# Solve's columns dealt out in turn over the partition groups, and SSD's dt moved into an exponent

## The chip, the cores and the metric

The kernel runs on one core of a Trainium2 chip. The metric is the device time of one execution in microseconds; lower is better. It is written in a tile language: the program text issues instructions to five engines (TensorE `pe`, ScalarE `act`, VectorE `dve`, GpSimd `pool`, SyncE `sp`, which issues the DMAs), and a scheduler puts the instructions of each engine in one queue, which the engine works off in order.

## The reference

One inference step of a hybrid layer on 1024 prompt rows and 64 sample rows (1088 in all), width 1024, all float32. What matters here are two of its parts. The gated DeltaNet (8 heads) solves, for each chunk of rows, a unit lower triangular system:

```
kk = einsum('bhik,bhjk->bhij', kh, kh)
lhs = where(strict, kk * dec * bt[..., :, None], 0.0) + eye
sol = triangular_solve(lhs, rhs, left_side=True, lower=True, unit_diagonal=True)
```

The Mamba-2 scan (SSD, 32 heads in 8 groups) weights each pair of rows i, j of a chunk by a decay and by dt of row j:

```
dec = exp(where(causal, gam_t[..., :, None] - gam_t[..., None, :], -inf))
w = cb[:, :, None] * dec * dt_t[..., None, :]
y = einsum('bghij,bjghp->bighp', w, xc)
```

The rest of the layer is an input projection (1024 to 12336 columns), causal convolutions, gates, two branch projections, an output projection, and a convolutional feed-forward part.

## The kernel before

Activations lie with channels on the 128 partitions and the 1088 rows along the free axis. Every projection is a loop over 128-column weight tiles; a weight is split into a high and a low part (`split`: ScalarE rounds `whi`, L114, VectorE subtracts to `wlo`, L115), and three matrix products per block of 128 are summed in PSUM, for three segments of 364 rows, in three rotating PSUM tiles `pj`.

The first part (to about 1560 us) weaves the input projections with the two scans. `weave` is a planner on the host: it keeps a model of TensorE's time in `now`, tasks that yield the latency (`LAT`) after which they may go on, and whenever no task is due it lets the main loop issue the next projection. TensorE's order is the order of the program text (`MAN`); the other engines' queues are ordered by the scheduler. Projections of q, k, v, x, B and C run through a convolution (`conv_steps`, VectorE L519 and L522, ScalarE L509, L517, L521); those of the gate z leave through `fz` (ScalarE L891, VectorE L893) to DRAM.

`decays` runs once: it makes dt (`dt8`, dt/8 for SSD), the negated cumulative decays `ngam` and derived tables, with ScalarE's Exp and Ln.

`gdn_inverse(h)` inverts one head's triangular matrices, 9 chunks of 128 rows with 4 diagonal blocks of 32 rows each, 36 blocks. The 32x32 diagonal blocks are inverted on VectorE, which this text calls Solve (L636 to L645): the blocks go through DRAM (`dU`) so that 108 partitions hold them, 3 groups of 36 partitions; each group works on 11 of the 33 columns (32 and one of padding) of all 36 blocks. For i from 1 to 31 one product (L640, `prod`) and one reduction (L643) make row i of the first n columns, n = min(i, 11). Then `XT` is a transposed copy (L645), written to DRAM as `dXT` (L648), read back into `NU` (L654), and transposed (L656, `prod` again). TensorE then combines the blocks (products from `prod`, `NU` and `Ub`, tile `n`). The planner counts 74 us for all of it (`LAT["solve"]`). `gdn_scan(h)` goes over the chunks one after the other: `r` (VectorE, L736), `u` (ScalarE, L742), the state `st` (L752), and `kd`, `vt` (ScalarE, L720, L721) for the next chunk.

`ssd_mix(g)` handles one group of four SSD heads, nine chunks. `decay` loads the decay rows into `gi`, masks them on GpSimd (L817) and takes four Exp of 128x128 into `E` with the row's `ngam` as bias (L820). `inputs` puts C'B and three transposes into one PSUM tile `sa`; VectorE multiplies E by it (L834), ScalarE copies the transposed B to `bt` (L836), and VectorE makes `xd` = x dt (L840) and `xw` = x wj (L841). TensorE sums xd'E and the state's part into `sy`, which VectorE reads for the new state (L872) and for `yc` (L878).

The later parts (branch projections, output projection, feed-forward) are not touched.

Of the kernel before, what the change touches and what calls it, by code (L numbers as in the profile page):

```python
# [15 lines left out]
AF = mybir.ActivationFunctionType  # L16
ALU = mybir.AluOpType
# [3 lines left out]
P = 128  # L21
# [26 lines left out]
def body(tc, I, O):  # L48
    nc = tc.nc
    ctx = ExitStack()  # L50
    pe, act, dve, pool, sp = nc.tensor, nc.scalar, nc.vector, nc.gpsimd, nc.sync
# [269 lines left out]
    with ExitStack() as c1:  # L321
# [111 lines left out]
        ngam = tl(c1p, [P, NC, 40], "ngam")  # L433
        beta = tl(c1p, [P, NC, 8], "beta")
        dt8 = tl(c1p, [P, NC, 32], "dt8")
# [11 lines left out]
        def decays():  # L447
            def tmp48(t):
                return t[:, 0:NC * 48].rearrange("p (c k) -> p c k", k=48)
            pz = tl(pp, [P, NC, 48], "n")  # L450
            for c in range(NC):
                tr(pz[:, c, :], zr[0:48, c * P:(c + 1) * P], ident[0:48, 0:48])
            zz, s1, s2, s3 = (tmp48(sgt(t)) for t in ("bm", "cm", "x0", "x1"))
            dve.tensor_scalar(out=zz[:, :, 0:8], in0=pz[:, :, 0:8], scalar1=-1.0, scalar2=None, op0=ALU.mult)
            dve.tensor_tensor(out=zz[:, :, 8:48], in0=pz[:, :, 8:48],
                              in1=bias40.unsqueeze(1).to_broadcast([P, NC, 40]), op=ALU.add)

            dve.scalar_tensor_tensor(out=s1, in0=zz, scalar=-1.0, in1=zz, op0=ALU.mult, op1=ALU.max)
            act.activation(s1, s1, AF.Exp, scale=-1.0)
            dve.tensor_scalar(out=s2, in0=s1, scalar1=1.0, scalar2=None, op0=ALU.add)  # L460
            act.activation(s3, s2, AF.Ln)
            dve.scalar_tensor_tensor(out=s1, in0=s2, scalar=-1.0, in1=s1, op0=ALU.add, op1=ALU.subtract)
            act.activation(s2, s3, AF.Exp, scale=-1.0)
            dve.tensor_tensor(out=s1, in0=s1, in1=s2, op=ALU.mult)
            dve.tensor_tensor(out=s3, in0=s3, in1=s1, op=ALU.subtract)
            dve.scalar_tensor_tensor(out=zz, in0=zz, scalar=0.0, in1=s3, op0=ALU.max, op1=ALU.add)
            act.activation(beta, zz[:, :, 0:8], AF.Exp, scale=-1.0)
            lga = tmp48(tl(gp, [P, TC], "E"))[:, :, 0:40]
            dve.tensor_tensor(out=lga, in0=zz[:, :, 8:48], in1=na.unsqueeze(1).to_broadcast([P, NC, 40]), op=ALU.mult)
            dve.memset(lga[64:128, 8, :], 0.0)  # L470
            dve.tensor_scalar(out=dt8, in0=zz[:, :, 16:48], scalar1=0.125, scalar2=None, op0=ALU.mult)
            yield LAT["dec2"]
            pg = tl(pp, [P, NC, 40], "sa")
            mm(pg, tri, lga, True, True)
            act.mul(ngam, pg, -1.0)
            yield 1.5
            pg = tl(pp, [P, NC, 40], "sy")
            mm(pg, sel, ngam, True, True)
            act.activation(ebl, pg, AF.Exp, scale=-1.0)
            dve.tensor_tensor(out=el, in0=ngam, in1=pg, op=ALU.subtract)  # L480
            act.activation(el, el, AF.Exp)
            dve.scalar_tensor_tensor(out=wj, in0=dt8, scalar=2.0, in1=el[:, :, 8:40], op0=ALU.mult, op1=ALU.mult)
            act.activation(neg, ngam[:, :, 0:8], AF.Exp, scale=-1.0)
            dve.tensor_scalar(out=neg, in0=neg, scalar1=-1.0, scalar2=None, op0=ALU.mult)
            grow = tl(gp, [P, TC], "NU", bufs=2)
            for (s, e), tag in zip(SEG9, ("gk", "gs", "sa")):
                pr = tl(pp, [P, 512], tag)
                for c in range(s // P, e // P):
                    tr(pr[0:40, c * P - s:(c + 1) * P - s], ngam[:, c, :], ident)
                act.copy(grow[0:40, s:e], pr[0:40, :384])  # L490
            sp.dma_start(gdr, grow[0:40, :])
# [102 lines left out]
        def gdn_inverse(h):  # L594
# [8 lines left out]
            for c0 in range(0, NC, 4):  # L603
                n = min(4, NC - c0)
                ps = tl(pp, [P, 4, P], "n")
                for c in range(c0, c0 + n):
# [16 lines left out]
                                     op0=ALU.mult, op1=ALU.mult)  # L623
# [10 lines left out]
            X = tl(gp, [108, 32, 11], "Xb")  # L634
            sp.dma_start(X, I["xinit"])
            for i in range(1, 32):  # L636
                n = min(i, 11)
                pr = tl(gp, [P, NC * 64], "prod")[0:108]
                prv = pr[:, 0:n * (i + 1)].rearrange("p (c j) -> p c j", j=i + 1)
                dve.tensor_tensor(out=prv, in0=X[:, 0:i + 1, 0:n].rearrange("p j c -> p c j"),  # L640
                                  in1=U[:, 0:i + 1, i:i + 1].rearrange("p j o -> p o j").to_broadcast([108, n, i + 1]),
                                  op=ALU.mult)
                dve.tensor_reduce(out=X[:, i, 0:n], in_=prv, axis=mybir.AxisListType.X, op=ALU.add)  # L643
            XT = tl(gp, [P, NC * 64], "prod")[0:108, 0:352].rearrange("p (c j) -> p c j", j=32)
            dve.tensor_copy(XT, X.rearrange("p j c -> p c j"))  # L645
            dXT = tl(dr, [NC * 4, 33, 32], "dXT", bufs=2)
            for g in range(3):
                sp.dma_start(dXT[:, 11 * g:11 * g + 11], XT[36 * g:36 * g + 36])  # L648
            dXv = dXT.rearrange("(c b) j i -> c b j i", b=4)

            Tl = tl(gp, [P, NC * 64], "prod").rearrange("p (c i) -> p c i", i=64)
# [155 lines left out]
        def ssd_mix(g):  # L807
# [3 lines left out]
            d4 = slice(4 * g, 4 * g + 4)  # L811

            def decay(c):
                gi = tl(sg, [P, 4, P], "gi", bufs=2)
                sp.dma_start(gi, gdr[h4, c * P:(c + 1) * P].partition_broadcast(P))
                E = tl(sg, [P, 4, P], "E", bufs=2)
                pool.affine_select(out=E, in_=gi, pattern=[[0, 4], [1, P]], compare_op=ALU.is_ge, fill=-NEG,  # L817
                                   base=0, channel_multiplier=-1)
                for a in range(4):
                    act.activation(E[:, a, :], E[:, a, :], AF.Exp, bias=ngam[:, c, 8 + 4 * g + a:9 + 4 * g + a], scale=-1.0)  # L820
                if c > 0:
                    act.activation(gi, gi, AF.Exp, scale=-1.0)
                    dve.scalar_tensor_tensor(out=gi, in0=chunk(cm, c).unsqueeze(1).to_broadcast([P, 4, P]),
                                             scalar=0.5, in1=gi, op0=ALU.mult, op1=ALU.mult)
                return gi, E

            def inputs(c, dec_c):

                gi, E = dec_c
# [7 lines left out]
                xd = tl(sg, [P, 4, 64], "xd", bufs=2)  # L837
                xw = tl(sg, [P, 4, 64], "xw", bufs=2)
                xv = ps[:, 2:4, :].rearrange("p a (b q) -> p (a b) q", q=64)
                dve.tensor_tensor(out=xd, in0=xv, in1=dt8[:, c, d4].unsqueeze(2).to_broadcast([P, 4, 64]), op=ALU.mult)  # L840
                dve.tensor_tensor(out=xw, in0=xv, in1=wj[:, c, d4].unsqueeze(2).to_broadcast([P, 4, 64]), op=ALU.mult)  # L841
                return gi, E, bt, xd, xw
            s8 = tl(sg, [P, 4, 64], "s8")
# [399 lines left out]
def layout(i):  # L1243
# [14 lines left out]
    def chans(a):  # L1258
# [5 lines left out]
    d = {  # L1264
        "ident": np.eye(P, dtype=np.float32),
        "tri": np.triu(np.ones((P, P), np.float32)),
        "xinit": np.tile(np.eye(32, 33, dtype=np.float32).reshape(1, 32, 3, 11).transpose(2, 0, 1, 3), (1, 36, 1, 1))
                   .reshape(108, 32, 11),
        "sel": np.concatenate([np.zeros((P - 1, P), np.float32), np.ones((1, P), np.float32)]),
        "xT": np.concatenate([g["x_prompt"][0], g["x_sample"][0]]).T.reshape(KT, P, T),  # L1270
# [61 lines left out]
```

## Time and profile before

| | |
|---|---|
| median of 3 runs | 2805.5 us (2805.27 to 2807.74) |
| the profiled execution | 2797.74 us, its span 2795.9 us |
| TensorE busy | 2728.5 us (98%), 18650 products |
| VectorE busy | 1868.0 us (67%), 3982 instructions |
| ScalarE busy | 1235.1 us (44%), 2813 instructions |
| GpSimd busy | 191.2 us (7%) |
| granted TensorE clock, mean | 0.996 of full speed |

The span runs from the first to the last instruction; the execution's own time has 1.8 us more around it. Busy time of TensorE is counted over pipelined products whose ends are modelled, so 98% does not mean that every cycle does work; what can be read safely is where TensorE stands idle and for whom. "Idle before, releaser" names the instruction whose end let a waiting one start. A number behind an arrow is the time waited.

### The profile page before, as it was taken

The numbers are of one execution on the slowest core, as the hardware profiler recorded it, in microseconds if no ns is written. First come the engines' busy times: TensorE is split into PE (matmuls) and PEld (weight loads), VectorE is DVE, ScalarE is ACT, GpSimd is POOL, SyncE is SP. The second block draws the span as 40 slices with busy tenths as digits, with TensorE's granted clock in tenths as the row PEclk, the third lists the DMA queues.
The fourth block names the chain that finished last, engine by engine and source line by source line (L and its number), as shares of the span: only waits on it lengthen the run. The fifth ranks groups of instructions, "written<-read, shape, count | busy, mean of one in ns | idle before, by whom it ended". The sixth has DMA issues, their size and how long they took to land.

```text
span 2795.9 us, 48799 instructions
## 1 busy us (share of the span) xinstructions
PE 2728.5 (98%) x18650; PEld 2639.7 (94%) x18650; DVE 1868.0 (67%) x3982; ACT 1235.1 (44%) x2813; POOL 191.2 (7%) x565
## 2 busy tenths in 40 slices
PE   6999999999999999999999999999999999999998
PEld 6999998999999999999999999999899999999998
DVE  5777679697887978877544557543666464555556
ACT  5634455454555545544443334222544242424244
POOL 0100001011110101101000000000000000000000
PEclk9999999999999999999999999999999999999999
DMA  6222323223231322323125755343211111111112
GB/s 228 95 67 88 112 68 107 79 79 106 71 120 61 110 76 84 100 76 107 65 92 202 262 188 185 122 144 93 87 53 46 46 41 43 46 42 50 39 61 73
DMA packets 204075, 266.72 MB, mean 95 GB/s; under 512 B 42490, under 2 KB 136378, under 8 KB 203842
## 3 DMA queue, kind: packets, MB, share of 16 engines
q1 hardware_dynamic: 203842, 263.62, 29.0%
q8 instruction: 146, 2.39, 0.3%
q14 instruction: 87, 0.71, 0.1%
HBM read 217.38 MB, written 46.13 MB: 94 GB/s over the span
## 4 chain that ended last, share of the span: by engine, by line
PE 81%; DVE 9%; DMA 5%; ACT 2%; issue 1%; POOL 1%; SPq 0%; DVEq 0%; POOLq 0%; ACTq 0%
PE pj L226 30%; PE pj L147 16%; PE sy L147 6%; PE sa L147 6%; PE gk L147 5%; PE gs L147 5%; PE sy L226 3%; DVE prod L640 2%; DMA gi<-gdr 2%; DVE Xb L643 2%; PE n L226 1%; DMA wada<-in_wada 1%; PE gk L226 1%; PE gs L226 1%; PE pj L1217 1%
## 5 line engine op out<-in xcount | busy, mean ns | idle before, releaser
L226 PE MATMUL pj<-h,whi 128*128 128x364 f32 x4560 | 1152.2, 334 | 5.8 <-DVE fz L893 5.8
L226 PEld LDWEIGHTS pj<-h,whi 128*128 128x128 f32 x4560 | 792.5, 189 | 13.5 <-DVE fz L893 7.0
L226 PE MATMUL pj<-h,wlo 128*128 128x364 f32 x2280 | 748.1, 328 | 3.8 <-DVE wlo L115 3.8
L147 PE MATMUL pj<-op,whi 128*128 128x364 f32 (+1 forms) x1904 | 476.7, 330 | 0.8 <-ACT op L188 0.6
L226 PEld LDWEIGHTS pj<-h,wlo 128*128 128x128 f32 x2280 | 429.0, 188 | 4.1 <-DVE wlo L115 4.1
L114 ACT CAST whi<-wraw 128x512 fp32r<-128x512 f32 (+1 forms) x382 | 231.2, 616 | 368.3 <-PE pj L147 130.7
L147 PEld LDWEIGHTS pj<-op,whi 128*128 128x128 f32 x1904 | 337.3, 188 | 6.7 <-issue 1.4
L115 DVE TENSOR_TENSOR wlo<-wraw,whi 128x512 fp32r<-128x512 f32 (+1 forms) x382 | 258.1, 685 | 102.2 <-ACT whi L114 101.4
L147 PE MATMUL pj<-op,wlo 128*128 128x364 f32 (+1 forms) x952 | 312.5, 329 | 0.0
L1124 DVE SCALAR_TENSOR_TENSOR acc<-buf,wfc,acc 128x364 f32<-128x364 f32 (+1 forms) x264 | 156.6, 597 | 96.5 <-ACT acc L1122 92.4
L147 PEld LDWEIGHTS pj<-op,wlo 128*128 128x128 f32 x952 | 178.8, 188 | 0.0
L147 PE MATMUL sy<-op,whi 128*128 128x364 f32 (+1 forms) x672 | 167.8, 330 | 0.0
L147 PE MATMUL gs<-op,whi 128*128 128x364 f32 (+1 forms) x652 | 164.1, 331 | 0.9 <-ACT q L1001 0.7
L147 PE MATMUL sa<-op,whi 128*128 128x364 f32 (+1 forms) x644 | 161.4, 330 | 0.0
L147 PE MATMUL gk<-op,whi 128*128 128x364 f32 (+1 forms) x640 | 159.5, 330 | 0.7 <-ACT op L114 0.7
L640 DVE TENSOR_TENSOR prod<-Xb,Ub 108x2 f32<-108x2 f32 (+30 forms) x248 | 129.2, 521 | 3.4
L820 ACT ACTIVATE E<-E,ngam 128x128 f32<-128x128 f32 x288 | 94.5, 394 | 74.2 <-POOL E L817 74.1
L147 PEld LDWEIGHTS sy<-op,whi 128*128 128x128 f32 x672 | 119.0, 188 | 1.0 <-issue 0.4
L147 PEld LDWEIGHTS gs<-op,whi 128*128 128x128 f32 x652 | 115.5, 188 | 3.1 <-ACT q L1001 0.9
L147 PEld LDWEIGHTS sa<-op,whi 128*128 128x128 f32 x644 | 114.0, 188 | 1.2 <-issue 0.6
L147 PEld LDWEIGHTS gk<-op,whi 128*128 128x128 f32 x640 | 113.3, 188 | 1.9 <-ACT op L114 1.0
L147 PE MATMUL sy<-op,wlo 128*128 128x364 f32 (+1 forms) x336 | 110.3, 328 | 0.0
(410 smaller groups left out, 4386.2 us busy)
## 6 DMA issues: line engine op xcount, KB each, us to landing
wraw<-in_win SPq DMA_DIRECT2D x158, 256.0 KB
wraw<-in_wup SPq DMA_DIRECT2D x88, 256.0 KB
gi<-gdr SPq DMA_DIRECT2D x72, 256.0 KB
wada<-in_wada SPq DMA_DIRECT2D x32, 512.0 KB
op<-spz SPq DMA_DIRECT2D x24, 544.0 KB
wraw<-in_wdown SPq DMA_DIRECT2D x40, 256.0 KB
spz<-fz SPq DMA_DIRECT2D x48, 182.0 KB
gt<-spg SPq DMA_DIRECT2D x48, 182.0 KB
```

What stands on the lines that cost most here:

```text
L114: act.copy(hi, src)
L115: dve.tensor_tensor(out=lo, in0=src, in1=hi, op=ALU.subtract)
L147: pe.matmul(pss[si][:, :e - s], lhsT=a[:, k, :], rhs=xk[:, b, s:e], start=(k == 0 and n == 0), stop=(k == nk - 1 and n == 2))
L226: pe.matmul(out, lhsT=lhsT, rhs=rhs, start=start, stop=stop)
L640: dve.tensor_tensor(out=prv, in0=X[:, 0:i + 1, 0:n].rearrange("p j c -> p c j"), in1=U[:, 0:i + 1, i:i + 1].rearrange("p j o -> p o j").to ...
L643: dve.tensor_reduce(out=X[:, i, 0:n], in_=prv, axis=mybir.AxisListType.X, op=ALU.add)
L820: act.activation(E[:, a, :], E[:, a, :], AF.Exp, bias=ngam[:, c, 8 + 4 * g + a:9 + 4 * g + a], scale=-1.0)
L1124: dve.scalar_tensor_tensor(out=acc[:, c0:c1], in0=buf[:, i + c0:i + c1], scalar=wfc[:, ti, i:i + 1], in1=acc[:, c0:c1], op0=ALU.mult, op1= ...
L1217: pe.matmul(pss[m - m0][:, :n], lhsT=wts[m][a][:, k, :], rhs=fs[k][:, b, s:e], start=(k == 0 and i == 0), stop=(k == 3 and i == 2))
```

## The change

Three things, in one file.

In Solve, the columns are dealt out in turn: group g of partitions holds columns g, g+3, g+6, ... in place of 11 neighbouring ones (`xinit`, the identity loaded into `X`, is laid out so, and `dXT` is written with a stride of three columns). Column c of the inverse begins at row c, so at step i the columns begun are the first third of i, rounded up, in each group: n = (i+2)//3.

In `decays`, ln(max(dt/8, 1e-37)) is made in a scratch tile (one VectorE operation, one Ln on ScalarE), and `dt8` is overwritten with ln(dt/8) + ngam after its last other use. In `ssd_mix` this sum is the bias of the Exp that makes E, so E carries dt.

With dt in E, `xd` is a plain copy of the transposed x, and moves from VectorE to ScalarE.

```
@@ decays
             dve.tensor_scalar(out=dt8, in0=zz[:, :, 16:48], scalar1=0.125, scalar2=None, op0=ALU.mult)
+            ldt = s2[:, :, 0:32]
+            dve.tensor_scalar(out=ldt, in0=dt8, scalar1=1e-37, scalar2=None, op0=ALU.max)
+            act.activation(ldt, ldt, AF.Ln)
             yield LAT["dec2"]
...
             dve.scalar_tensor_tensor(out=wj, in0=dt8, scalar=2.0, in1=el[:, :, 8:40], op0=ALU.mult, op1=ALU.mult)
+            dve.tensor_tensor(out=dt8, in0=ldt, in1=ngam[:, :, 8:40], op=ALU.add)
@@ gdn_inverse
             for i in range(1, 32):
-                n = min(i, 11)
+                n = (i + 2) // 3
...
-                sp.dma_start(dXT[:, 11 * g:11 * g + 11], XT[36 * g:36 * g + 36])
+                sp.dma_start(dXT[:, g:33:3], XT[36 * g:36 * g + 36])
@@ ssd_mix
-                    act.activation(E[:, a, :], E[:, a, :], AF.Exp, bias=ngam[:, c, 8 + 4 * g + a:9 + 4 * g + a], scale=-1.0)
+                    act.activation(E[:, a, :], E[:, a, :], AF.Exp, bias=dt8[:, c, 4 * g + a:4 * g + a + 1], scale=-1.0)
...
-                dve.tensor_tensor(out=xd, in0=xv, in1=dt8[:, c, d4].unsqueeze(2).to_broadcast([P, 4, 64]), op=ALU.mult)
+                act.copy(xd, xv)
@@ layout
-        "xinit": np.tile(np.eye(32, 33, dtype=np.float32).reshape(1, 32, 3, 11).transpose(2, 0, 1, 3), (1, 36, 1, 1))
+        "xinit": np.tile(np.eye(32, 33, dtype=np.float32).reshape(1, 32, 11, 3).transpose(3, 0, 1, 2), (1, 36, 1, 1))
```

TensorE's queue is the same in both kernels, row for row. VectorE loses the 72 rows of `xd` and gains two in `decays`; ScalarE gains 72 copies, one Ln and two table loads. In the changed file the lines from 472 on stand three lower, and those from 483 on four lower (L640 is L644 there). As the scheduler orders VectorE's and ScalarE's queues, other rows change places too. Three places:

VectorE, the end of the third head's Solve (`prod`, `Xb`), with the decay product `gi` of the next scan and the gate's `fz`. Before:

```order
L640 TENSOR_TENSOR prod_4817<-Xb_4728,Ub_4723 108x341
L643 TENSOR_REDUCE Xb_4728<-prod_4817 108x11
L696 TENSOR_TENSOR gi_5403<-gi_5403,q_4402 128x1024
L893 SCALAR_TENSOR_TENSOR fz_5463<-fz_5463,pj_5438 128x360
L640 TENSOR_TENSOR prod_4820<-Xb_4728,Ub_4723 108x352
L893 SCALAR_TENSOR_TENSOR fz_5502<-fz_5502,pj_5477 128x364
L643 TENSOR_REDUCE Xb_4728<-prod_4820 108x11
L697 TENSOR_TENSOR gi_5403<-gi_5403,q_4402 128x128
L645 COPY prod_4823<-Xb_4728 108x352
```

In the changed kernel:

```order
L644 TENSOR_TENSOR prod_4823<-Xb_4731,Ub_4726 108x352
L647 TENSOR_REDUCE Xb_4731<-prod_4823 108x11
L649 COPY prod_4826<-Xb_4731 108x352
L700 TENSOR_TENSOR gi_5406<-gi_5406,q_4405 128x1024
L897 SCALAR_TENSOR_TENSOR fz_5466<-fz_5466,pj_5441 128x360
L701 TENSOR_TENSOR gi_5406<-gi_5406,q_4405 128x128
L115 TENSOR_TENSOR wlo_5471<-wraw_5472,whi_5470 128x512
L897 SCALAR_TENSOR_TENSOR fz_5505<-fz_5505,pj_5480 128x364
```

The last steps of Solve and its copy now stand ahead of gi and of both fz, between which they stood.

VectorE, the end of the sixth head's Solve, with the convolution of B (`bm`), the split of the next weight (`wlo`) and `fz`. Before:

```order
L643 TENSOR_REDUCE Xb_10557<-prod_10649 108x11
L519 SCALAR_TENSOR_TENSOR bm_11126<-buf_11127,wcv_566,bm_11126 128x363
L645 COPY prod_10652<-Xb_10557 108x352
L893 SCALAR_TENSOR_TENSOR fz_11360<-fz_11360,pj_11335 128x364
L519 SCALAR_TENSOR_TENSOR bm_11126<-buf_11127,wcv_566,bm_11126 128x363
L115 TENSOR_TENSOR wlo_11297<-wraw_11298,whi_11296 128x512
L115 TENSOR_TENSOR wlo_11297<-wraw_11302,whi_11296 128x512
```

In the changed kernel:

```order
L649 COPY prod_10655<-Xb_10560 108x352
L700 TENSOR_TENSOR gi_11226<-gi_11226,q_10234 128x1024
L701 TENSOR_TENSOR gi_11226<-gi_11226,q_10234 128x128
L526 SCALAR_TENSOR_TENSOR bm_11129<-buf_11130,bm_11129 128x364
L115 TENSOR_TENSOR wlo_11300<-wraw_11301,whi_11299 128x512
L523 SCALAR_TENSOR_TENSOR bm_11129<-buf_11130,wcv_566,bm_11129 128x363
L897 SCALAR_TENSOR_TENSOR fz_11334<-fz_11334,pj_11309 128x364
L523 SCALAR_TENSOR_TENSOR bm_11129<-buf_11130,wcv_566,bm_11129 128x363
L115 TENSOR_TENSOR wlo_11300<-wraw_11305,whi_11299 128x512
```

The copy now stands ahead of gi (before, gi stood further up, among Solve's last steps); the first half of the split now stands ahead of two fz, both halves of it stood behind them.

ScalarE, a chunk of the fourth group: the copies out of `sa` and, behind them, the convolution's copy `buf` and the scan's u (written to a tile named `r`). Before:

```order
L521 ACTIVATE buf_6346<-q_6345 128x364
L836 COPY bt_6495<-sa_6489 128x128
L509 COPY buf_6346<-pj_6456 128x364
L742 ACTIVATE r_6546<-gs_6473,kn_4695 128x128
L517 ACTIVATE q_6345<-buf_6346,bcv_568,wcv_566 128x364
```

In the changed kernel:

```order
L525 ACTIVATE buf_6349<-q_6348 128x364
L840 COPY bt_6498<-sa_6492 128x128
L844 COPY xd_6500<-sa_6492 128x256
L513 COPY buf_6349<-pj_6459 128x364
L746 ACTIVATE r_6549<-gs_6476,kn_4698 128x128
```

The copy of xd has come in directly behind that of bt, ahead of u.

## Rows read from the trace of the kernel before

**Rows 1.** The page, part 1: busy us (share of the span) x instructions.

```profile
PE 2728.5 (98%) x18650; PEld 2639.7 (94%) x18650; DVE 1868.0 (67%) x3982; ACT 1235.1 (44%) x2813; POOL 191.2 (7%) x565
```

**Rows 2.** Waits of PE, 60 to 1560 us: us in total, times, longest.

```profile
PE pj L226 <- DVE fz L893: 5.8, 4, 2.4
PE sy L226 <- DVE yc L878: 4.3, 4, 1.4
PE gs L226 <- DVE r L736: 4.1, 7, 1.2
PE pj L226 <- DVE wlo L115: 3.8, 1, 3.8
PE n L226 <- ACT Ub L664: 1.9, 2, 1.4
PE n L226 <- DVE prod L656: 1.4, 2, 1.0
PE n L226 <- issue: 1.3, 1, 1.3
PE gs L226 <- ACT vt L721: 1.2, 2, 0.7
PE n L226 <- DVE NU L609: 0.9, 1, 0.9
```

**Rows 3.** Windows, the eight stretches of Solve: sum and mean of busy us.

```profile
sum 346.90, PE 336.03 PEld 320.93 DVE 333.06 ACT 179.86 POOL 63.37; mean PE 42.00 PEld 40.12 DVE 41.63 ACT 22.48 POOL 7.92
```

**Rows 4.** Groups of instructions by form, Solve: busy us, mean ns | idle before.

```profile
L640 DVE TENSOR_TENSOR prod<-Xb,Ub 108x352 f32<-108x352 f32 x8 | 6.6, 826 | 0.1
L640 DVE TENSOR_TENSOR prod<-Xb,Ub 108x143 f32<-108x143 f32 x8 | 3.3, 414 | 0.0
L643 DVE TENSOR_REDUCE Xb<-prod 108x11 f32<-108x352 f32 x8 | 4.1, 518 | 0.1
L643 DVE TENSOR_REDUCE Xb<-prod 108x11 f32<-108x143 f32 x8 | 2.4, 299 | 0.1
```

**Rows 5.** Timeline of SP, first and third head: start us, us, DMA issues.

```profile
139.06 1.83 SPq L628 DMA_DIRECT2D dU<-NU  x4
142.39 1.12 SPq L632 DMA_DIRECT2D Ub<-dU  x3
492.58 1.19 SPq L648 DMA_DIRECT2D dXT<-prod  x3
495.35 2.03 SPq L654 DMA_DIRECT2D NU<-dXT  x4
```

**Rows 6.** Groups by form: xd on DVE, two copies from PSUM on ACT.

```profile
L840 DVE TENSOR_TENSOR xd<-sa,dt 128x256 f32<-128x256 f32 x72 | 30.2, 420 | 6.0 <-ACT bt L836 5.8
L836 ACT COPY bt<-sa 128x128 f32<-128x128 f32 x72 | 19.2, 266 | 88.1 <-DVE E L834 83.1 <-DVE kn L620 4.3
L511 ACT COPY buf<-pj 128x296 f32<-128x296 f32 x55 | 22.0, 400 | 0.1
```

**Rows 7.** Waits of ACT, 60 to 1560 us.

```profile
ACT bt L836 <- DVE E L834: 83.1, 57, 2.8
```

**Rows 8.** Timeline, the scan's u on ACT and its reader on PE.

```profile
635.21 0.37 ACT L742 ACTIVATE r<-gs,kn 128x128 f32<-128x128 f32 x1 [0.41 <-PE gs L226]
636.97 0.38 PE L226 MATMUL gk<-r,kd 128*128 128x128 f32 x2
```

**Rows 9.** Timeline of ACT in `decays`.

```profile
76.71 1.28 ACT L461 ACT_TABLE_LOAD   x1
78.00 0.57 ACT L461 ACTIVATE x<-x 128x432 f32<-128x432 f32 x1
```

**Rows 10.** Timeline at the end of the third head's Solve, DVE and PE.

```profile
488.38 1.22 DVE L696 TENSOR_TENSOR gi<-gi,q 128x1024 f32<-128x1024 f32 x1
489.51 0.52 DVE L893 SCALAR_TENSOR_TENSOR fz<-fz,pj 128x360 f32<-128x360 f32 x1
490.09 0.60 PE L226 MATMUL pj<-h,whi 128*128 128x360 f32 x2 [2.40 <-DVE fz L893]
```

## Prediction

> **What bounds the kernel.** I read the page first. TensorE is busy 2728.5 of 2795.9 us, VectorE 67% and ScalarE 44% [rows 1]. So the kernel is bound by TensorE, and its 18650 matrix instructions stay as they are: row for row, TensorE's queue in the changed kernel is the old one. The change can move the time only through moments in which TensorE waits. So the second view is TensorE's waits in the stretch where both edited pieces run (60 to 1560 us): 24.7 us in all, by nine releasers [rows 2]. That is the whole stake, 0.9% of the time. By engine: VectorE ends 20.3 us of it (fz 5.8, yc 4.3, r 4.1, wlo 3.8, prod 1.4, NU 0.9), ScalarE 3.1 (Ub 1.9, vt 1.2), and 1.3 has no releaser.
>
> The third view asks whether VectorE is late because of Solve. Solve runs eight times, 43.4 us each on average from its first product to its last reduction. In these eight stretches VectorE is busy 333.06 of 346.90 us, 96%, while ScalarE has 52%; and TensorE is idle there 346.90 - 336.03 = 10.9 us [rows 3], 44% of the stake in 23% of the stretch. There VectorE is the engine that sets the pace, and a shorter Solve reaches TensorE. Elsewhere VectorE has room.
>
> **Solve.** A step i multiplies and reduces n columns of i+1 elements. Before, n = min(i, 11), 5522 elements a head over the 31 steps; now n = i/3 rounded up, 3817. The price comes from two sizes of each operation: the product takes 826 ns at 352 elements and 414 at 143, the reduction 518 and 299 [rows 4]. That is (826-414)/209 = 1.97 and (518-299)/209 = 1.05 ns an element, 3.02 together. 1705 elements fewer save 5.15 us a head, 41 us over eight; the 62 instructions a head stay. The serial path of a head shortens by the same 5.15 us.
>
> The result is now written in runs of 32 floats (128 bytes) where one run had 1408 bytes. A row with such short runs exists: the four writes of dU, also 128-byte runs. They are issued from 139.06 on for 1.83 us, and the reader of dU is issued at 142.39, 1.50 us after the last issue ended; for the old long-run write it is 495.35 - 492.58 - 1.19 = 1.58 us [rows 5]. Equal, so I take 0; even if the landing took twice as long, 1.6 us stand against 5.15 saved. Since Solve ends earlier, the 1.4 us of waits for its transposed blocks (prod in [rows 2]) go.
>
> **SSD's xd.** 72 products of 420 ns leave VectorE, 30.2 us. ScalarE copies 128x256 from PSUM instead; its copies take 266 ns at 128 columns (same tile) and 400 at 296 [rows 6], so 266 + 128 x 134/168 = 368 ns, 26.5 us in all. Three readers of one PSUM tile still come one after the other: ScalarE's copy of bt waits for VectorE's E product 57 times, 83.1 us in all [rows 7], and xw, on VectorE, now waits for bt and xd, where xd waited for bt. In the new order 16 of the 72 pairs of E and xw have nothing between them on VectorE; there the 0.37 us is lost again, 6 us. VectorE keeps 30.2 - 6 = 24 us; the bounds are 30.2 (all covered) and 30.2 - 26.5 = 3.7 (none covered). The Trainium skill (PSUM — Partial Sum Buffer, section on bank collisions) says that no two engines may access one PSUM bank at the same time in the same partitions, reads included, so that a dependency is put between them. The trace agrees (the 83.1 us), and by that rule alone, with every copy waited out, VectorE would keep 3.7 us, which would take my sum from -8.7 to about -8.
>
> ScalarE's extra copy stands, by the order, within two rows ahead of an operation of the GDN scan (u, kd, vt) in 54 of 72 cases. TensorE waits for those. In the row at 635.21 u takes 0.37 us and the product that reads it starts at 636.97, 1.4 us later [rows 8], and u is not among the nine releasers [rows 2]. A copy of 0.37 us fits into 1.4. Its cost lies between 0 and 26.5 us (every copy in TensorE's path); I take 1.0, near the low end, since u has been no releaser so far and vt only twice.
>
> **The decays.** ScalarE gets one Ln and two table loads of 1.28 us (the load at 76.71 is followed at 78.00 by the next operation [rows 9]), about 3.1 us; VectorE two small products, about 1 us. This comes once, near 84 us, where TensorE runs projections into three rotating PSUM tiles. Between 0 and 3.1 us on the path; I take 0.5. The Trainium skill (ScalarE: Activation LUTs, section What ACT_TABLE_LOAD costs) gives about 2.66 us a switch, its drain included. The row shows no idle time behind the load, so I stay with 1.28; by the page the upper bound would be 5.8 and my sum 0.4 us worse.
>
> **The sum.** What each line of waits loses:
> wlo 3.8 us, one wait, at the end of the sixth head's Solve: the split of the next weight stands behind Solve's copy in both orders, and 5.15 us less of Solve stand ahead of it, more than the wait; in the new order its first half stands ahead of the fz, too, but two gi rows have come in between. 3.0 goes.
> fz 5.8 us: the largest, ending at 490.09, waits for VectorE's fz at 489.51, which stands behind the last Solve rows and behind the gi product of 1.22 us [rows 10]. In the new order Solve is over before it, gi still stands ahead. A good half goes, 3.0.
> r and yc 8.4 us: their instructions stand behind one or two Solve instructions or behind E, xd and xw. VectorE's load in a Solve stretch falls from 41.6 us by 5.15 and by two or so of a group's nine xd, some 6.0 or 14%. Where an engine is 96% busy, waits fall by more than its load; I take a third, 2.8.
> prod 1.4: all goes.
> NU, Ub, vt and the one without releaser, 5.3 us: nothing.
> New: 1.0 + 0.5.
> -(3.0 + 3.0 + 2.8 + 1.4) + 1.5 = -8.7 us. The profiled execution took 2797.7 us (span 2795.9 and 1.8 around it), the median of the runs is 2805.5; the saving is the same in both, so 2796.8 for the median and a span near 2787.
>
> **Rivals.** A measurement of this kernel can tell some 0.2%, 5.6 us, from no change.
> *The waits only move.* The order within VectorE's queue is made anew: by the order, 15 of the fz and 11 each of yc and r change their places among their neighbours. If fz and r come to stand behind other long rows (gi 1.22 us, wlo, sq), the freed 65 us become idle time of VectorE and only prod and little else goes: -2 us, 2803.5. For it: more than half of TensorE's waits lie outside Solve's stretches. Against it: the 96% within. Chance 0.31.
> *All of VectorE's waits go*, since its queue is empty whenever TensorE needs it: -20.3 us, 2785.2. Against it: gi still precedes fz. Chance 0.08.
> *Slower: the copies of xd hold up the scan.* Each copy stands ahead of u, kd or vt; whenever ScalarE has no spare time then, TensorE loses 0.37 us. The gains without this term are 10.2 - 0.5 = 9.7 us, so 26 of 72 copies on the path break even and from 41 on the kernel is slower by over 5.6 us; all 72 give +16.8, 2822. For it: 54 of 72 stand there, and ScalarE waits 83.1 us ahead of bt, so xd also comes late. Against it: the 1.4 us, and no row of u among the waits. Chance 0.07.
>
> **The numbers.** My forecast, some 4 to 16 us faster, has what is left, 0.54. Faster by over 0.2%: 0.54 + 0.08 = 0.62; within 0.2%: 0.31; slower: 0.07. The range leaves out the lower half of the case in which all goes and the slower one: 2787 (-18.5) to 2807 (+1.5, every new cost at 3.1 us and only prod saved).
>
> **What would show it.** In the new profile Solve's two lines should hold 41 us less than before, VectorE about 1868 - 41 - 30 + 1 = 1798 us, ScalarE about 1235 + 27 + 3 = 1265, TensorE 2728 [rows 1]. TensorE's waits in 60 to 1560 us should sum to 13 to 19 us, with wlo and prod gone, fz about 3, r and yc about 5.5, and no line of u. Wrong would be: waits for u, kd, vt or E in a sum over 3 us (the slower rival); fz, r and yc as before although Solve has shrunk (the waits only moved); transposes that come no earlier after the last reduction (the short runs cost).

## The result, and the profile after

| | before | after |
|---|---|---|
| median of 4 runs each, us | 2805.39 (2799.89 to 2807.74) | 2785.89 (2784.52 to 2791.15) |
| ratio, with its 95% interval | | 0.9938 [0.9926, 0.9950] |
| the profiled execution, us | 2797.74 | 2791.15 |
| its span, us | 2795.9 | 2789.4 |
| waits of TensorE, 60 to 1560 us | 24.7 | 15.7 |

The kernel is 17.4 us faster by the ratio (14.0 to 20.8 by its interval), 19.5 by the two medians. The forecast was 8.7: the side is right, the size is half of what was measured. The spans of the two profiled executions stand only 6.5 us apart, and the section behind the experiments says why.

Part 1 of the page of the kernel after, which answers to [rows 1]:

```profile
PE 2726.9 (98%) x18650; PEld 2638.5 (95%) x18650; DVE 1815.0 (65%) x3912; ACT 1257.5 (45%) x2888; POOL 185.5 (7%) x565
```

TensorE's work is the same, and VectorE lost 53 us of busy time. The waits of PE in 60 to 1560 us, after (waited for: us in total, times, longest), to be laid beside [rows 2]:

```profile
PE gs L226 <- DVE r L740: 6.4, 10, 1.2
PE gk L226 <- ACT r L746: 3.0, 3, 2.0
PE n L226 <- issue: 2.5, 2, 1.5
PE pj L226 <- DVE fz L897: 1.6, 2, 1.2
PE gs L226 <- ACT vt L725: 1.3, 2, 1.0
PE n L226 <- DVE NU L613: 0.9, 1, 0.9
```

Four releasers are gone (yc 4.3, wlo 3.8, Ub 1.9, prod 1.4) and fz fell from 5.8 to 1.6. But r rose from 4.1 to 6.4, the waits without a releaser from 1.3 to 2.5, and u, which had no line before, has one of 3.0 (it writes the tile `r`, so it stands there as ACT r). The sum fell by 9.0.

The groups of instructions of Solve on VectorE and of the copies from `sa`, after (busy us, mean ns of one | idle before, releaser), beside [rows 4, 6]:

```profile
L644 DVE TENSOR_TENSOR prod<-Xb,Ub 108x2 f32<-108x2 f32 (+30 forms) x248 | 103.8, 419 | 3.8
L647 DVE TENSOR_REDUCE Xb<-prod 108x1 f32<-108x2 f32 (+30 forms) x248 | 69.2, 279 | 4.3
L845 DVE TENSOR_TENSOR xw<-sa,wj 128x256 f32<-128x256 f32 x72 | 30.2, 419 | 9.7 <-ACT xd L844 9.7
...
L844 ACT COPY xd<-sa 128x256 f32<-128x256 f32 x72 | 27.3, 379 | 0.0
L840 ACT COPY bt<-sa 128x128 f32<-128x128 f32 x72 | 19.1, 265 | 75.1 <-DVE E L838 74.1
```

Solve's two groups hold 173.0 us; before, the same two lines held 129.2 and 83.4. That is 39.6 less (41 was forecast). The copy takes 379 ns (368 forecast), and xw now waits 16 times for it.

The windows of the eight stretches of Solve, after (their sum, and the mean busy us), which answer to [rows 3]:

```profile
sum 296.10, PE 287.72 PEld 272.52 DVE 279.73 ACT 151.92 POOL 54.41; mean PE 35.96 PEld 34.07 DVE 34.97 ACT 18.99 POOL 6.80
```

A stretch has 37.0 us where it had 43.4. VectorE is still busy in 94% of it, and TensorE idles 8.4 us in all eight where it idled 10.9. So only 2.5 of the 9.0 us of waits went within the stretches. Most of the rest went just behind them: the waits of TensorE in the 20 us behind each stretch sum to 8.0 us before and 1.6 after. VectorE now needs some 6 us less for a stretch. At the end of the sixth head's Solve, VectorE made the two halves of the next weight's wlo here before (start us, us, engine line op):

```profile
984.71 1.30 DVE L115 TENSOR_TENSOR wlo<-wraw,whi 128x512 fp32r<-128x512 f32 x2
```

The first half ended at 985.41, and the product that had waited 3.8 us for it started at 985.46. The timeline of VectorE at the same place, after:

```profile
971.23 0.54 DVE L647 TENSOR_REDUCE Xb<-prod 108x11 f32<-108x352 f32 x1
971.66 0.61 DVE L523 SCALAR_TENSOR_TENSOR bm<-buf,wcv,bm 128x364 f32<-128x364 f32 x1
972.17 0.83 DVE L649 COPY prod<-Xb 108x352 f32<-108x352 f32 x1
972.90 1.23 DVE L700 TENSOR_TENSOR gi<-gi,q 128x1024 f32<-128x1024 f32 x1
974.04 0.30 DVE L701 TENSOR_TENSOR gi<-gi,q 128x128 f32<-128x128 f32 x1
974.24 0.54 DVE L526 SCALAR_TENSOR_TENSOR bm<-buf,bm 128x364 f32<-128x364 f32 x1
974.69 0.70 DVE L115 TENSOR_TENSOR wlo<-wraw,whi 128x512 fp32r<-128x512 f32 x1
```

This is the place of the old wlo wait, the longest of all. The first wlo now starts at 974.69, 2.9 us after the last reduction ended, and is over at 975.38; the same product starts at 978.99 and does not wait. These rows show a second thing: each instruction starts 0.1 us before the one ahead of it is over (971.23 + 0.54 = 971.77, the next starts at 971.66). Durations in a row add up to more than the engine's time. Over the whole span these overlaps sum to 185.9 us before and 172.6 after. That is 13.3 of the 16.8 us by which VectorE's busy time fell less (53 us) than its two groups did (39.6 and 30.2); the other rows grew by 3.6 us.

### The profile page after: what moved, and what is told of

Same layout as the page of the kernel before. It is cut to its first block, busy times and chain, and to the rows that moved or that the text cites. A ratio compares the mean times of both kernels' runs of the same rounds, so it can differ in the third digit from the quotient of the medians.

```text
span 2789.4 us, 48767 instructions
## 1 busy us (share of the span) xinstructions
PE 2726.9 (98%) x18650; PEld 2638.5 (95%) x18650; DVE 1815.0 (65%) x3912; ACT 1257.5 (45%) x2888; POOL 185.5 (7%) x565
## 3 DMA queue, kind: packets, MB, share of 16 engines
q1 hardware_dynamic: 212482, 263.62, 30.2%
q8 instruction: 146, 2.39, 0.4%
## 4 chain that ended last, share of the span: by engine, by line
PE 88%; DVE 5%; DMA 4%; ACT 1%; issue 1%; SPq 0%; POOL 0%; DVEq 0%; ACTq 0%; POOLq 0%
PE pj L226 36%; PE pj L147 16%; PE sy L147 6%; PE gk L147 5%; PE gs L147 5%; PE sa L147 5%; PE sy L226 3%; PE gk L226 2%; DMA wada<-in_wada 2%; PE n L226 2%; PE gs L226 1%; DVE prod L644 1%; DMA gi<-gdr 1%; PE pj L1221 1%; DVE Xb L647 1%
## 5 line engine op out<-in xcount | busy, mean ns | idle before, releaser
L824 ACT ACTIVATE E<-E,dt 128x128 f32<-128x128 f32 x288 | 94.6, 396 | 80.1 <-POOL E L821 80.0
L147 PE MATMUL gs<-op,wlo 128*128 128x364 f32 (+1 forms) x326 | 107.7, 330 | 0.0
```

Of the source, the lines that this page charges most:

```text
L147: pe.matmul(pss[si][:, :e - s], lhsT=a[:, k, :], rhs=xk[:, b, s:e], start=(k == 0 and n == 0), stop=(k == nk - 1 and n == 2))
L824: act.activation(E[:, a, :], E[:, a, :], AF.Exp, bias=dt8[:, c, 4 * g + a:4 * g + a + 1], scale=-1.0)
```

## The experiments

The theory: only Solve's 40 us matter; they shorten waits of TensorE behind Solve, and the copy of xd on ScalarE brings nothing. Its rivals: the xd part carries a share; the short DMA runs give some of the gain back; and, since the gain is twice the forecast, a wait of TensorE costs more than its length. All ratios are to the kernel before, timed beside each kernel.

### Both kernels once more

> The kernel before, unchanged, for a second profile. If the gain of the change is TensorE's waits in the woven part (60 to 1560 us) alone, these waits again sum to 23 to 27 us here. If half of the measured gain (17 us, against 9 us of waits that went) is chance in parts that the change does not touch, the times of this kernel spread by 5 us or more and the profile differs from the first one behind 1560 us by as much. If a wait costs more than its length because TensorE's granted clock falls behind a long one, the profile shows rows of half clock behind the longest waits in the woven part, and fewer of them in the changed kernel.

Measured: 1.0004 [0.9994, 1.0013], 25.4 us of waits. The eleven runs of this kernel lie between 2794.3 and 2803.7 us.

> The changed kernel, unchanged, for a second profile and a tighter interval. Waits only: a ratio of 0.996 to 0.998 and waits of 14 to 18 us in the woven part. Waits and the clock behind them: 0.992 to 0.996, with fewer rows of half clock in the woven part than the kernel before has. Chance outside: the ratio leaves its first interval of 0.9926 to 0.9950 upwards.

Measured: 0.9950 [0.9938, 0.9962], 2785.70 us against 2798.97; 15.3 us of waits. The gain repeats, as 14.0 us by the ratio (10.6 to 17.4). The second pair of profiles agrees with the first on the waits (25.4 to 15.3 where it was 24.7 to 15.7), but the spans are now 13.7 us apart, where they were 6.5. Waits alone do not fix the time. What else differs shows in the timeline of PE in the second profile of the kernel before, around one of its waits:

```profile
320.20 0.33 PE L226 MATMUL pj<-h,wlo 128*128 128x364 f32 x1
320.36 0.50 PE L226 MATMUL pj<-h,whi 128*128 128x364 f32 x2
320.70 0.33 PE L226 MATMUL pj<-h,wlo 128*128 128x364 f32 x1
320.96 0.24 PE L226 MATMUL n<-prod,NU 32*32 32x32 f32 x2
323.59 0.75 PE L226 MATMUL n<-prod,NU 32*32 32x32 f32 x34 [2.39 <-DVE prod L656]
324.27 0.60 PE L226 MATMUL pj<-h,whi 128*128 128x364 f32 x2
324.71 0.39 PE L226 MATMUL pj<-h,wlo 128*128 128x364 f32 x1
324.90 0.81 PE L226 MATMUL pj<-h,whi 128*128 128x364 f32 x2
325.51 0.50 PE L226 MATMUL pj<-h,wlo 128*128 128x364 f32 x1
```

Three products of a block start within 0.50 us ahead of the wait (320.20 to 320.70) and within 0.80 behind it (324.71 to 325.51). The windows of the same profile (window, its length, busy time of the engines with instructions in brackets, then PEclk, the granted clock):

```profile
300.00:324.00 24.00, 20.93 (x161) 20.01 (x162) 16.80 (x32) 13.85 (x37) 5.52 (x8) 1.00 0.53 163
324.00:328.50 4.50, 4.50 (x36) 4.46 (x31) 2.03 (x5) 1.26 (x3) 0.00 (x0) 0.62 0.56 195
```

The granted clock falls from 1.00 to 0.62 on average: by the trace's clock records it stands at 0.5 (1.2 GHz, where 1.00 is 2.4) for 3.4 us from 324.8 on, and then at 1.00 again. This profile has three such stretches in the woven part, behind the waits of 2.39 (prod), 3.79 (wlo) and 2.28 us (fz). The second profile of the kernel after has none.

A profile is one execution, but the mean granted clock of every timed run is on record. Over the 32 runs of the kernel before that were timed here it is 0.9949 in the mean, over the nine of the kernel after 0.9966. What is missing to 1.00, times the span of the run, is 14.4 and 9.6 us. So I estimate from these that the clock gives some 5 us of the gain in a mean run.

### Each part alone

Solve's part alone, on the kernel before:

```
-                n = min(i, 11)
+                n = (i + 2) // 3
-                sp.dma_start(dXT[:, 11 * g:11 * g + 11], XT[36 * g:36 * g + 36])
+                sp.dma_start(dXT[:, g:33:3], XT[36 * g:36 * g + 36])
-        "xinit": ....reshape(1, 32, 3, 11).transpose(2, 0, 1, 3)
+        "xinit": ....reshape(1, 32, 11, 3).transpose(3, 0, 1, 2)
```

> Only Solve's columns are dealt out in turn; xd stays a product on VectorE and the exponent as it was. Theory: Solve carries the gain, since VectorE sets the pace in its eight stretches: VectorE 38 to 42 us less busy, TensorE's waits 15 to 19 us in the woven part, time 8 to 14 us below the kernel before. Rival: moving xd off VectorE carries at least half, and this one gains 2 to 6 us only.

Measured: 0.9942 [0.9929, 0.9955], 2783.12 us, waits 9.4 us. The gain of 16 us is larger, and the waits are fewer, than was expected.

The other part alone (the exponent, and xd as a copy on ScalarE), which is the kernel after with these three lines of Solve as before (the third is `xinit`):

```
-                n = (i + 2) // 3
+                n = min(i, 11)
-                sp.dma_start(dXT[:, g:33:3], XT[36 * g:36 * g + 36])
+                sp.dma_start(dXT[:, 11 * g:11 * g + 11], XT[36 * g:36 * g + 36])
...
```

> Only dt in the exponent of E with the copy of xd on ScalarE; Solve as before. Theory: VectorE loses 30 us and waits some 10 us longer for ScalarE ahead of xw, TensorE's waits 20 to 25 us, time 0 to 5 us below the kernel before. Rival: this part carries half of the gain, 7 to 10 us. Second rival: ScalarE's copies hold up the scan, waits for u and vt of 5 us and more, time 1 to 5 us above the kernel before.

Measured: 0.9991 [0.9982, 0.9999], 2796.33 us, waits 23.3 us. The five largest waits of PE in 60 to 1560 us, exponent alone:

```profile
PE gs L226 <- DVE r L740: 5.0, 8, 1.1
PE pj L226 <- DVE fz L897: 3.5, 4, 1.4
PE gk L226 <- ACT r L746: 3.3, 3, 1.5
PE sy L226 <- DVE yc L882: 2.6, 2, 1.6
PE gs L226 <- ACT vt L725: 2.0, 4, 0.9
```

And those of Solve's part alone, where the same lines have the numbers of the old file:

```profile
PE sy L226 <- DVE yc L878: 2.5, 2, 1.4
PE gs L226 <- DVE r L736: 1.5, 3, 0.8
...
PE gk L226 <- ACT r L742: 0.2, 1, 0.2
```

Solve's part carries the whole gain. The exponent's part brings 2.6 us (0.3 to 5.0): it takes waits from yc, fz and wlo (1.1 us of it are left) and hands them to u (3.3 where the kernel before has none), r and vt. No wait of 2 us is left in the woven part of its profile, and its eleven runs have a mean clock of 0.9962, which by the reckoning above is 3.7 us better than the kernel before: the clock alone can account for its gain. Together with Solve's part it costs 6 us of waits (15.3 against 9.4), and in time nothing that can be told (2785.70 against 2783.12, intervals overlapping).

### Who pays for the copy on ScalarE

The kernel after, with the copy of xd on VectorE:

```
-                act.copy(xd, xv)
+                dve.tensor_copy(xd, xv)
```

> The changed kernel, but the copy of xd stays on VectorE. It tells why the exponent part adds some 6 us of TensorE's waits to dealt-out columns alone (15.3 against 9.4 us). Theory: ScalarE's copy does, since xw on VectorE waits for it ahead of r, and u stands behind it on ScalarE: here the waits for u go, those for r fall from 6.7 to 1 to 4 us, the sum is 9 to 11 us and the time that of solve_only within 2 us. Rival: the order of VectorE's queue, made anew, does: the sum stays at 13 to 17 us and the time at that of after_again.

Measured: 0.9939 [0.9926, 0.9951], 2783.86 us, waits 11.9 us, between the two expectations: r 3.3, u 0.4, where the kernel after has 6.4 and 3.0. VectorE takes back 30.2 us of rows and TensorE waits less. So some 3.6 of the 6 us of waits that the exponent's part adds come from where the copy runs; the other 2.5 stay open. In time the two places of the copy can't be told apart. In the kernel after, the timeline of GpSimd, ScalarE and TensorE at u's longest wait reads:

```profile
264.58 0.63 POOL L821 TENSOR_SCALAR_AFFINE_SELECT E<-gi 128x512 f32<-128x512 f32 x1 [14.69 <-DMA gi<-gdr]
265.25 1.28 ACT L824 ACTIVATE E<-E,dt 128x128 f32<-128x128 f32 x4 [3.48 <-POOL E L821]
266.43 0.61 ACT L826 ACTIVATE gi<-gi 128x512 f32<-128x512 f32 x1
266.95 0.35 ACT L746 ACTIVATE r<-gs,kn 128x128 f32<-128x128 f32 x1
...
267.35 0.49 PE L226 MATMUL gk<-r,kd 128*128 128x128 f32 x2 [2.02 <-ACT r L746]
```

u (L746) stands behind the four Exp of E and the Exp of gi, not behind a copy of xd. In Solve's part alone the scheduler puts u straight behind E's Exp, ahead of gi's, and the wait here is 0.2 us. So at this place the copy's own 0.38 us costs nothing, and the queue's new order costs the 0.5 us of gi's Exp. Most of the 2.02 us lies ahead of that: E's Exp waited 3.48 us for GpSimd's mask, which had waited for the load of the decay rows. In the second profile of the kernel after, with the same order, u's wait here is 0.98 us. At the other places the runs do not part the order from the copy.

The product xw on GpSimd, from xd in SBUF, so that VectorE need not wait for the copy:

```
-                dve.tensor_tensor(out=xw, in0=xv, in1=wj[:, c, d4].unsqueeze(2).to_broadcast([P, 4, 64]), op=ALU.mult)
+                pool.tensor_tensor(out=xw, in0=xd, in1=wj[:, c, d4].unsqueeze(2).to_broadcast([P, 4, 64]), op=ALU.mult)
```

> The changed kernel with xw made by GpSimd from the copy of xd in SBUF, so that VectorE reads the tile sa once only: a version that could beat both. If VectorE's wait for ScalarE ahead of xw (9.7 us, 16 times) and xw's 30 us hold up r, TensorE's waits for r fall from 6.7 to 1 to 3 us, and the time is 2 to 6 us below after_again. Rival: GpSimd's queue, which waits for the decay rows of the next chunks, brings xw late: TensorE waits in sy for GpSimd, 5 us or more, and the time is above that of after_again.

Measured: 0.9951 [0.9938, 0.9963], 2786.60 us, waits 14.8 us, as the kernel after; neither the gain nor the rival's waits for GpSimd in sy came. The group of xw on GpSimd in this kernel (busy us, mean ns | idle before):

```profile
L845 POOL TENSOR_TENSOR xw<-xd,wj 128x256 f32<-128x256 f32 x72 | 52.0, 722 | 256.4 <-ACT xd L844 256.4
```

and its two largest waits of PE in 60 to 1560 us:

```profile
PE gs L226 <- DVE r L740: 7.9, 13, 2.2
PE gs L226 <- ACT vt L725: 3.8, 4, 1.9
```

VectorE is freed of 30.2 us of rows and of all its waits for xd, and r is still later than before. So a wait of VectorE for the copy is not shown to make r late, and my guess that it did has not held. What does is open; that some of it goes when the copy sits on VectorE is all that the runs show. In the kernel after, rows of Solve stand among the three rows of VectorE ahead of r at nine of its ten waits, and xw at two.

### Solve's size, and its short runs

In these two the exponent is left as in the kernel before. The first writes `dXT` in long runs again, with the columns still dealt out, so that they land in wrong places of the inverse:

```
-                sp.dma_start(dXT[:, g:33:3], XT[36 * g:36 * g + 36])
+                sp.dma_start(dXT[:, 11 * g:11 * g + 11], XT[36 * g:36 * g + 36])
```

> As solve_only, but dXT is written in runs of 1408 bytes as before, so that columns land in the wrong places of the inverse: the price of the 128-byte runs by themselves. Theory: the short runs make the readers of dXT some 1.8 us later after the first write was issued (4.6 against 2.8 us), but the blocks come ahead of TensorE's need, so this kernel has 2.8 us there and the time of solve_only within 2 us. Rival: the short runs give back part of the gain, and this one is 3 us or more below solve_only.

Measured: 0.9935 [0.9922, 0.9949], 2783.25 us, against 0.9942 with short runs: no difference that can be told; waits 12.4 us. But with short runs the path is longer. The timeline of SP, the third head, in the kernel after:

```profile
485.88 2.49 SPq L652 DMA_DIRECT2D dXT<-prod  x3
...
490.50 2.77 SPq L658 DMA_DIRECT2D NU<-dXT  x4
```

and with long runs:

```profile
486.25 1.12 SPq L648 DMA_DIRECT2D dXT<-prod  x3
...
489.39 2.37 SPq L654 DMA_DIRECT2D NU<-dXT  x4
```

SP needs 2.49 us to issue the three writes where it needed 1.12 (1.19 in [rows 5]). Over all eight heads the reader is issued 4.55 us after the first write begins, in the median, against 2.65. So the short runs cost 1.9 us of the 5 us that Solve saves on its path, and no wait hangs on them: prod is among the releasers of neither.

The second works on one column of each group alone:

```
-                n = (i + 2) // 3
+                n = 1
```

> As solve_only, but each step works on one column alone and leaves out the others: what would be left if Solve cost nearly nothing. Solve's two lines should hold some 85 us (62 instructions a head near the smallest duration, 0.17 us) in place of 173. Theory: the first 40 us of Solve paid for most, since waits need VectorE to be full; TensorE's waits go from 9.4 to 5 to 8 us and the time to 2 to 5 us below solve_only. Rival: the gain goes on with VectorE's load at the same rate, 10 us or more below solve_only. Second rival: what is left is not Solve's, no difference.

Measured: 0.9925 [0.9913, 0.9938], 2780.23 us, waits 10.5 us. Solve's groups hold 93.3 us, 80 less than after, and that brings some 3 to 5 us more. The waits did not fall to the 5 to 8 us expected, so what these 3 to 5 us are made of is not shown. The first 40 us were worth 14 to 17. There is little left to win in Solve.

### What a wait costs

Ten waits put into the kernel after, two products of TensorE with a chain of small copies on VectorE between them, ahead of projections near the end of the woven part. The short chain has 3 copies:

```
...
+                    d = tl(pp, [P, P], "n")
+                    pe.matmul(d, lhsT=ident, rhs=ident, start=True, stop=True)
+                    dve.tensor_copy(t0, d[:, 0:8])
+                    for _ in range(2):
+                        dve.tensor_copy(t1, t0)
+                        t0, t1 = t1, t0
+                    d = tl(pp, [P, P], "n")
+                    pe.matmul(d[0:8, :], lhsT=t0, rhs=ident, start=True, stop=True)
...
```

> The changed kernel with ten short waits of TensorE put in among the last merge projections, where it otherwise does not wait (some 1340 to 1560 us): a product, a chain of three small copies on VectorE, a product of the result. Each wait should last 0.7 to 1.1 us, with what it adds itself some 10 us in all. Theory (a long wait costs more than its length since the granted clock falls behind it): no stretch of half clock behind waits this short, the time 8 to 12 us above the changed kernel. Rival (the clock has nothing to do with waits): the same here.

Measured: 1.0023 [1.0014, 1.0032], 2809.37 us, some 20 us or more above the kernel after, where 8 to 12 were expected. The long chain has 15 copies (`range(14)`):

> The same ten waits with a chain of fifteen copies: 2.5 to 4 us each, 25 to 40 us in all. Theory: most of them are followed by a stretch of half clock of 3.4 us or more, which costs 1.7 us or more each, so that the time rises by the sum of the waits and another 12 to 25 us. Rival: the time rises by the sum of the waits, within 4 us, and half clock is no more frequent than with short waits.

Measured: 1.0201 [1.0185, 1.0218], 2859.62 us. Both chains took longer than I had meant, and the short one was followed by half clock twice. The waits of PE in 1300 to 1640 us, short chain:

```profile
PE n L914 <- DVE ct L911: 12.4, 8, 2.7
```

and long chain:

```profile
PE n L914 <- DVE ct L911: 48.9, 10, 7.9
```

The windows of the stretch with these waits (PEclk is the third number from the end), short chain, long chain, and the second profile of the kernel after:

```profile
1340.00:1575.00 235.00, 220.79 (x1424) 211.11 (x1424) 97.48 (x234) 82.63 (x203) 6.76 (x16) 0.99 0.36 117
```

```profile
1340.00:1620.00 280.00, 230.76 (x1391) 219.55 (x1390) 110.78 (x350) 79.82 (x199) 6.97 (x16) 0.90 0.28 91
```

```profile
1340.00:1555.00 215.00, 213.84 (x1408) 208.10 (x1408) 94.10 (x198) 83.13 (x206) 6.91 (x16) 1.00 0.42 140
```

The granted clock falls with the waits: 1.00 without, 0.99 and 0.90 with them. From the same product to the same product (from 1340.2 to 1620.1 in the short kernel) the long one needs 50.0 us more. Its waits are 34.3 us longer. It stands 41.3 us at half clock outside its waits, the short one 6.4; half of the difference is 17.5. Together 51.8, for 50.0 measured. Nine of the ten waits of the long kernel last 4.2 to 7.9 us, the tenth 0.2. So the clock adds some 2.3 us (20.7 over nine) to each of the nine, beside their length. In the short kernel eight of the ten show as waits for the chain, and only the two longest (2.39 and 2.67 us) have such a stretch behind them, those of 1.69 and below have none. Over the same products the short kernel needs 25.1 us more than the second profile of the kernel after: 13.5 of waits, 3.2 by half clock, and 8.4 of the rest, in which the put-in products are.

With this the ten profiles of kernels with the same TensorE instructions can be reckoned up. Each is taken from the same product (at 60 us) to the same product (at 1550.1 in the first profile), and a stretch at half clock is charged with half of its length outside waits (waits of over 0.2 us are counted):

| profile | elapsed | waits | half clock, outside waits | rest |
|---|---|---|---|---|
| before | 1490.0 | 24.7 | 5.3 | 1462.7 |
| before, again | 1492.5 | 25.2 | 10.1 | 1462.3 |
| exponent alone | 1487.2 | 23.3 | 0 | 1463.9 |
| after | 1478.7 | 15.7 | 3.4 | 1461.3 |
| after, again | 1475.4 | 14.1 | 0 | 1461.3 |
| Solve alone | 1473.1 | 9.3 | 3.4 | 1462.1 |
| copy on VectorE | 1474.8 | 11.5 | 3.4 | 1461.6 |
| long runs | 1474.3 | 11.4 | 3.4 | 1461.2 |
| one column | 1470.7 | 10.2 | 0 | 1460.5 |
| xw on GpSimd | 1480.7 | 14.1 | 6.8 | 1463.2 |

The rest is 1462 us to within 2 in all of them, though the elapsed times differ by 22. So the woven part's time is made of work, waits and clock, and nothing else moves it by more than 3.4 us. The Trainium skill (TensorE: Matmul & The Clock Gate, section HAM oscillation — how this bites in real kernels) charges a throttled stretch with half of its length; by that rule the table closes, without it the rest would scatter over 7 us in place of 3.4.

Of the waits of 2 us and more in these ten profiles and the one with short waits, 7 of 10 have a half-clock stretch that starts at their end or within 2 us of it; of those from 1.25 to 2 us, 6 of 39. No half-clock stretch in the woven part lies elsewhere. The nine long waits of the long chain all have one, from within the wait or just behind it. The length of a wait alone does not decide it: one of 1.29 us in Solve's part alone is followed by such a stretch, one of 1.30 us with the copy on VectorE and one of 2.44 us in the kernel before are not.

## Why the prediction was right, and where it was off

The term by term reckoning, waits in us, first pair of profiles and second pair:

| term | predicted | first pair | second pair |
|---|---|---|---|
| wlo | -3.0 | -3.8 | -3.8 |
| fz | -3.0 | -4.2 | -3.7 |
| r and yc | -2.8 | -2.0 | -1.3 |
| prod | -1.4 | -1.4 | -3.3 |
| NU, Ub, vt, no releaser | 0 | -0.6 | -0.7 |
| new: u, decays, op | +1.5 | +3.0 | +2.7 |
| sum of waits | -8.7 | -9.0 | -10.1 |
| the same, up to the product at 1550 | | -9.0 | -11.1 |
| half clock behind waits | not in the sum | -0.9 | -5.0 |
| rest | | -1.4 | -1.0 |
| elapsed, by the table above | | -11.3 | -17.1 |

**Right.** That the gain comes through TensorE's waits: its instructions are the same and the rest of the table stays within 3.4 us. Solve's price from two sizes, 41 us, against 39.6. That wlo and prod go, and fz by more than half. The waits in all: 15.7 and 15.3, within the 13 to 19 named. That their sum came within 0.3 us in the first pair is in part luck: its terms were off by 0.6 to 1.5 us, and the errors cancelled: wlo and fz lost more than forecast, r with yc less, and the new waits are twice those forecast. The time itself lies past the 4 to 16 us of the main case; by the ratio it is 2788 us, just within the range, by its median of 2785.9 just below it.

**The step that failed** is the unit of the sum. It took "waits lost" for time saved, one to one. A long wait of TensorE can be followed by 3.4 us or more at half clock, as 7 of 10 waits of 2 us and more were, which costs 1.7 us or more beside the wait itself; and the change removed most of the long ones: of waits of 2 us and more the two profiles of before have 6, those of after 1. The trace of before showed it: in its woven part 6.8 us at half clock lie at the wlo wait. How much the clock gave differs from execution to execution, 0.9 us in one pair and 5.0 in the other; the exponent alone, with nearly the waits of before, had none in its profile; over the timed runs it is some 5 us. Three things make up the miss: waits 0.3 to 2.4 us more than forecast, clock 0.9 to 5.0, rest 1.0 to 1.4. The mean of the two pairs is 14.2 us, and the intervals of the two measurements meet from 14.0 to 17.4. Behind 1550 us, where the kernels issue the same instructions, the ten profiles scatter between 1235.9 and 1241.2 us without an order that follows the change (the kernel after has 1241.2 and 1238.5, the kernel before 1236.5 and 1235.9); the first after-profile lost 4.7 there, 3.2 of it in waits of TensorE (the longest, 3.0 us, for a load of the weight `wada`), and so its span shows only 6.5.

**r and u.** The sum let r fall and u be none. yc went altogether (-4.3), but r rose by 2.3 and u took 3.0. The argument for u, that 1.4 us lie between it and its reader [rows 8], looked at one place; u's longest wait is at 267 us, where it stands behind two other rows of ScalarE's queue. The rule that I had set for the slower rival (u, kd, vt or E over 3 us in sum) was met in the first profile, at 4.3 with vt (2.3 in the second), and yet the kernel is faster, since that rival's price of 26 copies on the path is far off.

**xd.** VectorE was to keep 24 us of the 30.2. The wait for bt at xd [rows 6] is now a wait for the copy at xw, 9.7 us instead of 6.0, so VectorE gave 3.7 us back and kept 26.5. The Trainium skill (PSUM — Partial Sum Buffer, section PSUM bank collisions raise a hardware error) has a dependency put between two engines that touch one bank in the same partitions, reads included; the trace agrees, with bt behind E for 74.1 us and xw behind xd for 9.7. But at 56 of the 72 copies VectorE does not wait, so the lower bound of the prediction, with every copy waited out, is far from what came. None of it reached TensorE: with the copy on VectorE the kernel is as fast.

**The short runs** were priced at 0 because [rows 5] showed equal times from the last issue to the reader's. The row was read for the landing alone; the issue itself, 1.37 us more a head, was left out. So the sign that the prediction named for this came: at the third head the reader is issued 5.5 us after the last reduction (485.01 to 490.50), where it was 3.7 (491.63 to 495.35). No wait of TensorE hangs on it.

**The decays** cost TensorE nothing: neither kernel has a wait from 60 to 119 us.

**Busy times.** VectorE has 1815 us where 1798 were named, ScalarE 1257.5 where 1265 were: rows of durations overlap at their ends, as shown above.

**Rivals.** The waits did not only move, and not all of VectorE's went: r, fz and NU still hold 8.9 us. By the time alone the second of these, at -20.3 us, lies nearer to the measured 17.4 than the forecast does; only the waits tell them apart.

## What to carry to other kernels

Where TensorE sets the time, sum the waits of TensorE, not the busy time of the engine that is made faster, and look for them behind the serial piece, not only within it. Price a long wait of TensorE at more than its length: look at the granted clock right behind it, and take the long ones out first. Work that is moved from one busy engine to another, and into the queue ahead of a scan, must be timed alone: here half of the edit earned the whole gain.

The best of the versions run are within each other's intervals: Solve's part alone (0.9942), and the kernel after with the copy on VectorE (0.9939), against 0.9938 and 0.9950 for the kernel after. None is shown to beat it; Solve's part alone does the same with three edited lines.

## What was not expected of the hardware

- A wait of TensorE of 1.29 us can be followed by 3.4 us at 1.2 GHz, and one of 2.44 us by none; with nine waits of 4.2 to 7.9 us the mean granted clock of their stretch fell to 0.90.
- Three DMA writes with runs of 128 bytes took SP 2.50 us to issue where three with runs of 1408 bytes took 1.13 (medians of eight heads each).
- Instructions of VectorE that follow each other without a wait overlap by 0.1 us in the records (the rows above), so 39.6 us less in Solve's groups and 30.2 us less of xd, 69.8 in all, gave 53 us of engine time; 13.3 us of the difference are such overlaps.
